# A weave-planned encoder layer on one core: four operations of the second token sums moved into the first Strassen product and from GpSimd to VectorE, one weight remainder moved to VectorE, sample tiles of the retention counted as ready 1.6 planner units later

## The chip, the cores and the metric

The kernel runs on one core of a Trainium2 chip. The metric is device time in microseconds (us), the median of the runs. The core has five engines that run side by side and meet at semaphores: TensorE (PE, matmuls; PEld is its weight load), VectorE (DVE), ScalarE (ACT), GpSimd (POOL) and SyncE (SP, which issues most DMAs). Each engine works through its own queue in order: an instruction that waits holds up everything behind it on that engine.

## The reference, cut to what matters

One layer of a streaming encoder, for 1024 prompt tokens and 32 sample tokens with the same weights:

```
h  = x @ w_in                      # attention q/k/v, indexer, retention q/k/v/gate, two branch gates
A  = sparse attention of h         # top-k keys per query by an indexer score, softmax, times v
R  = retention of h                # rotary q/k, per chunk: scores, state update, group norm, swish gate
m  = sigmoid(g_A) * (A @ w_pa) + sigmoid(g_R) * (R @ w_pr)
x1 = LN(alpha*x + m @ w_o)
y  = LN(alpha*x1 + (silu(x1 @ w_gate) * (x1 @ w_up)) @ w_down)
```

Matmuls run in a rounded fp32 form on operands that are split into a high part and a remainder (`split`, L144): high by ACT, remainder by DVE or POOL as `src - high`.

## The kernel before, in words

**Order of the work.** The order of TensorE's instructions is written out by the kernel. A main stream (a generator of matmuls) is walked by the class `Weave` (L51); side streams, spawned on the way, are let in between two matmuls once the planner's clock `W.t` has reached the time that they asked for. The clock counts planned costs only: a matmul of n columns costs max(256, n)/2400 units (384 columns 0.16, 288 columns 0.12, 512 columns 0.213), and `W.on(engine, cost, after)` books a slot on an engine and returns its end plus a lag (0.3 for ACT, 0.4 for POOL; for DVE 1.6 in this stage). The order on DVE, ACT and POOL is made by the framework's scheduler from program order, readiness and free tile buffers.

**Retention** (`ret_job`, L678). For four weight groups p and nine token tiles t (t = 8 is the sample tile of 32 tokens) the main stream makes one projection (L182 to L198) and spawns `ret_tile` (L560). A prompt tile's projection is copied by ACT (L693), and its ready time is the end of that copy. A sample tile's is merged by ACT and DVE (L201 to L207), and its ready time is only `W.t + 0.2`. `ret_tile` then has four operations of POOL (rotary, L574 to L577) and its steps on PE. These are the times that it asks for:

```
yield 0.0, W.on("p", 2.4, t_ev) + 2.2              # L578, ahead of the transposes L580, L581
yield 0.22, W.on("a", 0.65, W.t + 0.22) + 1.2      # ahead of the scores, L593
yield 0.43, max(W.on("v", 0.5, W.t + 0.43) + 1.0, state_t.get(p, 0.0))   # ahead of L604 to L610
yield c, tt + 5.0                                  # c = 1.3; ahead of the last transposes, L642
```

**Gate projections as filler** (`g_jobs`, L702). 16 blocks b of three chunks (384, 384 and 288 columns, 24 matmuls each, L172) follow the retention as main stream. The weights of block b + 1 are loaded and split when block b begins; block 0's remainder is made by DVE, the others' by POOL. At the start of a chunk, when no side stream is left, `to_attention` (L743) opens the attention, whose two streams are spawned at the start of a later chunk (`t_go = W.t + 1.5`). From then on the gate chunks fill PE between the steps of the attention. Block 15 is kept until the attention has ended.

**Feed-forward.** The first pair of gate and up blocks is made plainly (`u_plain`, L1141), in two halves u of the tokens (264 columns each). All others are made as seven Strassen products for each half (`products`, L1204, 12 matmuls each, numbered z = 0 to 6). The right sides are sums of token blocks, made once by `sums(u)` (L1116): for each of four slices k it forms four block sums and four differences, and splits four results into `tq[2]`, `tq[3]`, `tq[1]` and `T4` (which overwrites the block `B12`). It uses the tiles `e1`, `u2`, `u3`, with two buffers each, which `products` uses for its own evictions too. The block sum of `B21` is made by POOL into a tile `ts` with one buffer (L1121). `sums(0)` runs while `u_plain` is in its second half; all of `sums(1)` follows it, and `products(q, 0, ...)` and `products(q, 1, ...)` come behind that. In `products` the bank of z = 0 is written again by z = 4, after ACT's copy of `e1` (L1222); that of z = 2 by z = 5, after the eviction L1226; that of z = 3 by z = 6. The products of half 1 read `tq[2]`, slice by slice, from z = 1 on.

Of the kernel before, what the change touches and what calls it, by code (L numbers as in the profile page):

```python
# [10 lines left out]
F32 = mybir.dt.float32  # L11
# [3 lines left out]
ALU = mybir.AluOpType  # L15
# [7 lines left out]
HALF, SUB = 528, 264  # L23
# [81 lines left out]
def body(ctx, tc, nc, a):  # L105
# [20 lines left out]
    def f32(ap):  # L126
        return ap.bitcast(F32)

    def dma(out, in_):
        nc.sync.dma_start(f32(out) if out.dtype == F32R else out, f32(in_) if in_.dtype == F32R else in_)  # L130
# [9 lines left out]
    ring1 = Open("ring1", bufs=4)  # L140
# [3 lines left out]
    def split(hi, lo, src, hi_eng="pool", lo_eng="pool"):  # L144
        if hi_eng == "pool":
            nc.gpsimd.tensor_scalar(hi, src, 1.0, 1.0, op0=ALU.mult, op1=ALU.mult)
        elif hi_eng == "act":
            nc.scalar.activation(hi, src, AF.Copy)  # L148
        else:
            nc.vector.tensor_copy(hi, src)  # L150
        e = nc.gpsimd if lo_eng == "pool" else nc.vector
        e.tensor_tensor(lo, src, f32(hi), op=ALU.subtract)  # L152

    def unit(src, p, hi_eng="act", lo_eng="pool"):
        raw = ring1.tile([128, 1024], F32, name="raw", bufs=2)
        dma(raw, src)
        hi = p.tile([128, 1024], F32R, name="whi")
        lo = p.tile([128, 1024], F32R, name="wlo")
        split(hi, lo, raw, hi_eng, lo_eng)
        return hi, lo  # L160

    def blk(u, n=128):
        return tuple(w.rearrange("p (k c) -> p k c", c=n) for w in u)
# [92 lines left out]
    for c0, n in CHUNKS:  # L256
        for k in range(KT):
            for w, raw, i, k0 in ((w0, raws[0], 2, k), (w1, raws[1], 0, k - 1)):
                if c0 == 0 and k0 in pieces:
                    s = slice(pieces[k0][0] * 128, pieces[k0][1] * 128)  # L260
# [22 lines left out]
    ks = ip.tile([128, 1568], F32R, name="iks")  # L283
# [226 lines left out]
    st = {}  # L510

    def load_pair(p, u):
        rg = ring2 if p in (1, 3) else ring1
        src = a["wv"][u] if p == 0 else a["wr"][p - 1, u]
        units.setdefault(p, []).append(blk(unit(src, rg, lo_eng="pool" if p < 2 else "dve"), 512))
# [162 lines left out]
    def ret_job():  # L678
        for p in range(4):
            for t in range(9):  # L680
                if p == 3 and t == 1:
                    ring2.close()
                    st["hA"] = Open("headA")
                if p == 3 and 1 <= t < 6:
                    load_head(0, t - 1)
                if p < 3 and t < 4:
                    load_pair(p + 2, t)
                    W.on("v", 1.2, W.on("a", 0.95, W.t + 0.5))
                qkv = rp.tile([128, 512], F32, name="qkv", bufs=3)
                src = yield from nat_tile(units[p + 1], t, rp, qkv)  # L690
                t_ev = W.t + 0.2
                if t < 8:
                    nc.scalar.activation(qkv, src, AF.Copy)  # L693
                    t_ev = W.on("a", 0.5, W.t)
                    src = qkv
                W.spawn(ret_tile(p, t, src, t_ev))
            units.pop(p)

# [3 lines left out]
    def g_jobs():  # L702
        w = blk(unit(a["wT"][19], ring1, lo_eng="dve"))
        for b in range(16):
            cur = w
            if b < 15:
                w = blk(unit(a["wT"][20 + b], ring1, lo_eng="dve" if b < 1 else "pool"))
            dd = ga_d[b] if b < 8 else gr_d[b - 8]
            for c0, n in CHUNKS:
                if "att" not in st and not W.sides and b >= PRE:  # L710
                    to_attention()
                    t_go = W.t + 1.5
                elif "att" in st and st["go"] and W.t >= t_go:
                    for z in st["go"]:
                        W.spawn(z)
                    st["go"] = None
                if b == 16 - POST and c0 == 0:
                    c_units.append(blk(unit(a["w_pr"][0], ring1)))
                    c_units.append(unit(a["w_pa"][0], ring1))
                while b >= 16 - POST and "rt" not in st:  # L720
                    yield 0.2
                o = gbank()
                yield from tform(o, cur, KT, xr(c0, n), n)
                g = gv.tile([128, 384], F32, name="gev", bufs=2)
                if "rt" in st:
                    nc.vector.tensor_copy(g[:, :n], o[:, :n])
                    dma(dd[:, c0:c0 + n], g[:, :n])
                else:
                    nc.scalar.activation(g[:, :n], o[:, :n], AF.Copy)
                    nc.scalar.dma_start(dd[:, c0:c0 + n], g[:, :n])  # L730
                W.on("a", 0.4, W.t)
# [283 lines left out]
    op = Open("wo", side="right")  # L1015
# [66 lines left out]
    B11, B12, B21, B22 = x1[0][0], x1[0][1], x1[1][0], x1[1][1]  # L1082
# [30 lines left out]
        for i in range(2):  # L1113
            split(hi[:, i], lo[:, i], v[:, i], "act", "dve")

    def sums(u):  # L1116
        s = slice(u * SUB, (u + 1) * SUB)
        for k in range(4):
            a_, b_, c_ = (st["up"].tile([128, SUB], F32, name=nm, bufs=2) for nm in ("e1", "u2", "u3"))
            d_ = st["up"].tile([128, SUB], F32, name="ts", bufs=1)  # L1120
            nc.gpsimd.tensor_tensor(d_, f32(B21[0][:, k, s]), f32(B21[1][:, k, s]), op=ALU.add)  # L1121

            def whole(out, b):
                nc.vector.tensor_tensor(out, f32(b[0][:, k, s]), f32(b[1][:, k, s]), op=ALU.add)

            def cut(t, src):
                split(t[0][:, k, s], t[1][:, k, s], src, "act", "dve")

            whole(a_, B11)
            whole(b_, B12)  # L1130
            nc.vector.tensor_tensor(a_, b_, a_, op=ALU.subtract)
            whole(c_, B22)
            nc.vector.tensor_tensor(b_, c_, b_, op=ALU.subtract)
            nc.vector.tensor_tensor(c_, c_, a_, op=ALU.subtract)
            cut(tq[2], c_)
            cut(tq[3], b_)
            cut(tq[1], a_)
            nc.vector.tensor_tensor(c_, d_, c_, op=ALU.subtract)
            cut(T4, c_)

    def u_plain():  # L1141
        ws = [(went_of(a["w_gate"][f]), went_of(a["w_up"][f])) for f in range(2)]
        sg = hg.tile([128, 2, TT], F32, name="sg", bufs=2)
        while len(W.sides) > 4:
            yield 0.2
        for u in range(2):
            if u == 1:
                while W.sides:
                    yield 0.2
                ynp.close()  # L1150
                st["tset"] = Open("tset")
                for z in range(1, 4):
                    tq[z] = [st["tset"].tile([128, 4, HALF], F32R, name=f"T{z}{i}") for i in range(2)]
                st["up"] = Open("up", side="right")
                sums(0)
                st["quad"] = make(*seq[0])
            s = slice(u * SUB, (u + 1) * SUB)
            for f in range(2):
                wg, wu = (blk(w) for w in ws[f])
                for h in range(2):  # L1160
                    d = sg[:, f, h * HALF + u * SUB:h * HALF + (u + 1) * SUB]

                    def rx(k):
                        b = x1[k // 4][h]
                        return b[0][:, k % 4, s], b[1][:, k % 4, s]
                    pg, pu = mbank(), mbank()
                    yield from tform(pg, wg, KT, rx, SUB)
                    nc.scalar.activation(d, pg[:, :SUB], AF.Silu)
                    yield from tform(pu, wu, KT, rx, SUB)
                    nc.vector.tensor_tensor(d, pu[:, :SUB], d, op=ALU.mult)  # L1170
        sums(1)
        st["quad"].more()
        st["quad"].last()
        store_h(sg, 0)
# [77 lines left out]
    def u_jobs():  # L1252
        nxt = st["quad"]
        for x, (m, f) in enumerate(seq):
            q = nxt
            if m == 0:
                sg = hg.tile([128, 2, TT], F32, name="sg", bufs=2)
            if x + 1 < len(seq):
                nxt = make(*seq[x + 1])
                hooks = {1: nxt.more, 3: nxt.last}  # L1260
            else:
                first.append(went_of(a["w_down"][0]))
                first.append(went_of(hd_d[0], "dve"))
                hooks = {1: lambda: first.append(went_of(a["w_down"][1])),
                         3: lambda: first.append(went_of(hd_d[1], "dve"))}
            yield from products(q, 0, sg, m == 0, {})
            yield from products(q, 1, sg, m == 0, hooks)
            if m == 1:
                store_h(sg, 2 * f)
# [206 lines left out]
```

## Time and profile before

| what | value |
|---|---|
| median of 3 runs | 1900.14 us (1900.13 to 1900.14) |
| profiled execution, its own time | 1900.51 us |
| span of that execution, first to last instruction | 1898.9 us |
| PE, DVE, ACT, POOL busy | 98%, 68%, 38%, 40% |
| mean granted TensorE clock | 0.994 of full speed |

A busy PE is one with a matmul in its pipeline. A timeline row gives start, duration, engine, line, operation and tiles, and in brackets how long the engine stood idle before it and what released it. A windows row gives the length of a stretch, each engine's busy time with its instructions, the granted clock as a share of full speed, and the DMA's share.

### The profile page before, as it was taken

The page shows a single profiled execution, that of the slowest core. Times are in us where ns is not written, and L with a number is a line of the kernel's source. Part 1 is how long each engine was busy: PE and PEld are TensorE (multiplying, and loading weights), DVE is VectorE, ACT ScalarE, POOL GpSimd, SP SyncE. Part 2 cuts the span into 40 slices and gives each one's busy share as a digit, 9 for nine tenths or more (in the row PEclk, how much of TensorE's full clock was granted, in tenths as well). Part 3 has the DMA queues.
Part 4 walks back from the last instruction along what each step waited for, and adds up shares of the span by engine and source line. Part 5 has one row for each costly group of instructions (what it writes and reads, how often), then busy time and mean ns, then how long its engine had stood idle before and what let it go on. Part 6 is the DMA issues. An engine that isn't in the chain of part 4 may idle for free. (4 is left out here: it accounts for less than half of the span.)

```text
span 1898.9 us, 31028 instructions
## 1 busy us (share of the span) xinstructions
PE 1859.0 (98%) x11361; PEld 1688.2 (89%) x11361; DVE 1298.4 (68%) x2693; ACT 715.1 (38%) x1495; POOL 751.8 (40%) x787
## 2 busy tenths in 40 slices
PE   8999999999999999999999999899999999999998
PEld 8999899787888999998999879899999999877776
DVE  4599889999995776676533378754555555476667
ACT  5443322423333555555522255432333332432212
POOL 5445633455545544543321133243343333462211
PEclk9999999999999999999999999999999999999999
DMA  5335742223334756551845662212222222642212
GB/s 189 113 128 196 266 138 86 65 73 98 87 86 125 195 144 171 143 145 52 273 146 155 186 199 84 67 68 67 80 96 71 75 82 90 203 165 89 83 40 91
DMA packets 154367, 233.11 MB, mean 123 GB/s; under 512 B 18960, under 2 KB 118280, under 8 KB 154216
## 3 DMA queue, kind: packets, MB, share of 16 engines
q1 hardware_dynamic: 147736, 223.03, 37.6%
q10 hardware_dynamic: 6480, 8.11, 1.3%
q8 instruction: 89, 1.46, 0.3%
q14 instruction: 62, 0.51, 0.1%
HBM read 164.79 MB, written 67.48 MB: 122 GB/s over the span
## 5 line engine op out<-in xcount | busy, mean ns | idle before, releaser
L152 POOL TENSOR_TENSOR wlo<-raw,whi 128x1024 fp32r<-128x1024 f32 (+2 forms) x83 | 196.1, 2367 | 337.8 <-ACT whi L148 295.2
L148 ACT ACTIVATE whi<-raw 128x1024 fp32r<-128x1024 f32 (+1 forms) x158 | 137.1, 881 | 183.8 <-PE m L1218 33.7
L172 PE MATMUL g<-xh,whi 128*128 128x384 f32 (+1 forms) x600 | 198.2, 330 | 0.0
L172 PE MATMUL g<-xl,whi 128*128 128x384 f32 (+1 forms) x600 | 198.1, 330 | 0.0
L172 PE MATMUL g<-xh,wlo 128*128 128x384 f32 (+1 forms) x600 | 197.9, 330 | 0.0
L377 DVE MAX8 m<-sc 128x8 f32<-128x384 f32 (+6 forms) x209 | 182.2, 874 | 4.7
L378 DVE MATCH_REPLACE8 sc<-m,sc 128x384 f32<-128x384 f32 (+6 forms) x209 | 180.0, 862 | 0.1
L778 POOL TENSOR_TENSOR P<-TB,mask 128x512 f32<-128x512 f32 (+3 forms) x112 | 99.1, 913 | 120.9 <-PE m L842 98.3
L172 PEld LDWEIGHTS g<-xl,whi 128*128 128x128 f32 x600 | 113.5, 189 | 3.0 <-issue 0.9
L172 PEld LDWEIGHTS g<-xh,wlo 128*128 128x128 f32 x600 | 113.5, 189 | 2.4 <-issue 0.5
L172 PEld LDWEIGHTS g<-xh,whi 128*128 128x128 f32 x600 | 113.5, 189 | 2.2
L1315 DVE TENSOR_TENSOR yo<-m,yo 128x512 f32<-128x512 f32 x128 | 85.4, 686 | 43.5 <-PE m L172 42.1
L1218 PE MATMUL m<-T,whi 128*128 128x264 f32 x624 | 114.6, 283 | 0.0
L172 PE MATMUL g<-whi,xl 128*128 128x512 f32 x256 | 104.9, 410 | 0.0
L172 PE MATMUL g<-whi,xh 128*128 128x512 f32 x256 | 104.4, 408 | 0.0
L172 PE MATMUL g<-wlo,xh 128*128 128x512 f32 x256 | 104.4, 408 | 0.0
L1218 PEld LDWEIGHTS m<-T,whi 128*128 128x128 f32 x624 | 96.6, 188 | 0.0
L172 PE MATMUL m<-rT,whi 128*128 128x384 f32 (+1 forms) x384 | 90.7, 322 | 0.0
L1218 PE MATMUL m<-T,wlo 128*128 128x264 f32 x312 | 88.6, 284 | 0.0
L1218 PE MATMUL g<-x,whi 128*128 128x264 f32 x416 | 79.2, 287 | 5.6 <-ACT e L1222 5.6
L1218 PE MATMUL m<-x,whi 128*128 128x264 f32 x416 | 78.5, 287 | 1.2 <-DVE u L1226 0.7
L152 DVE TENSOR_TENSOR wlo<-raw,whi 128x512 fp32r<-128x512 f32 (+1 forms) x81 | 69.6, 872 | 14.0 <-ACT whi L148 13.1
(333 smaller groups left out, 5493.4 us busy)
## 6 DMA issues: line engine op xcount, KB each, us to landing
raw<-wT SPq DMA_DIRECT2D x33, 512.0 KB, 3.7
raw<-w_gate SPq DMA_DIRECT2D x22, 512.0 KB, 3.4
raw<-w_up SPq DMA_DIRECT2D x22, 512.0 KB, 3.4
hd<-sg SPq DMA_DIRECT2D x22, 512.0 KB, 3.2
raw<-w_down SPq DMA_DIRECT2D x22, 512.0 KB, 3.5
raw<-hd SPq DMA_DIRECT2D x22, 512.0 KB, 3.6
raw<-wr SPq DMA_DIRECT2D x16, 512.0 KB, 4.2
ml<-mtd SPq DMA_DIRECT2D x16, 512.0 KB, 4.5
```

Of the source, the lines that this page charges most:

```text
L148: nc.scalar.activation(hi, src, AF.Copy)
L152: e.tensor_tensor(lo, src, f32(hi), op=ALU.subtract)
L172: nc.tensor.matmul(out, lhsT=l, rhs=r, start=i == 0, stop=i == m - 1)
L377: nc.vector.max(m8[0:n], v)
L378: nc.vector.match_replace(v, m8[0:n], v, TAKEN)
L778: nc.gpsimd.tensor_tensor(pp[0:n, n0:n0 + nn], TB[0:n, b0 + n0:b0 + n0 + nn], masks[t][0:n, n0:n0 + nn], op=ALU.add)
L1218: nc.tensor.matmul(o, lhsT=w[l][:, k, :], rhs=b[r][:, k, s], start=z < 4 and k == 0 and j == 0, stop=k == 3 and j == 2, skip_group_check=True)
L1315: nc.vector.tensor_tensor(y, src, y, op=ALU.add)
```

## The change

The sample tiles' ready time in the retention is counted 1.6 units later. The remainder of gate block 1's weights is made by DVE. `sums` takes a list of slices; the sum of `B21` is made by DVE into the tile `u2`, which is free by then, and `ts` is gone (for both halves). `sums(1)` makes slices 0 and 1 ahead of the first Strassen product; slices 2 and 3 are issued in the first product of half 0, behind its evictions z = 1 and z = 2.

```diff
                     src = qkv
+                else:
+                    t_ev += 1.6
                 W.spawn(ret_tile(p, t, src, t_ev))
...
-                w = blk(unit(a["wT"][20 + b], ring1, lo_eng="dve" if b < 1 else "pool"))
+                w = blk(unit(a["wT"][20 + b], ring1, lo_eng="dve" if b < 2 else "pool"))
...
-    def sums(u):
+    def sums(u, ks=range(4)):
         s = slice(u * SUB, (u + 1) * SUB)
-        for k in range(4):
+        for k in ks:
             a_, b_, c_ = (st["up"].tile([128, SUB], F32, name=nm, bufs=2) for nm in ("e1", "u2", "u3"))
-            d_ = st["up"].tile([128, SUB], F32, name="ts", bufs=1)
-            nc.gpsimd.tensor_tensor(d_, f32(B21[0][:, k, s]), f32(B21[1][:, k, s]), op=ALU.add)
...
             cut(tq[1], a_)
-            nc.vector.tensor_tensor(c_, d_, c_, op=ALU.subtract)
+            whole(b_, B21)
+            nc.vector.tensor_tensor(c_, b_, c_, op=ALU.subtract)
             cut(T4, c_)
...
-        sums(1)
+        sums(1, range(2))
...
-            yield from products(q, 0, sg, m == 0, {})
+            yield from products(q, 0, sg, m == 0, {z: (lambda k=z: sums(1, [k + 1])) for z in (1, 2)} if x == 0 else {})
             yield from products(q, 1, sg, m == 0, hooks)
```

## Rows read from the trace of the kernel before

**Rows 1.** The page: the span, and the busy time of the engines.
```profile
span 1898.9 us, 31028 instructions
PE 1859.0 (98%) x11361; PEld 1688.2 (89%) x11361; DVE 1298.4 (68%) x2693; ACT 715.1 (38%) x1495; POOL 751.8 (40%) x787
```

**Rows 2.** The waits of PE over the whole span, the two longest: who waited for whom, us in total, times, longest.
```profile
PE m L580 <- POOL qk L577: 5.8, 3, 2.8
PE g L1218 <- ACT e L1222: 5.6, 1, 5.6
```

**Rows 3.** The timeline of PE in the retention, at the transposes of the sample tiles of p = 0, 1 and 3 (the matmuls of 32x32), with two matmuls of the main stream in a row ahead of the second.
```profile
378.16 0.24 PE L580 MATMUL m<-ident,qk 32*128 32x32 f32 x1 [1.08 <-POOL qk L577]
...
445.80 0.39 PE L172 MATMUL g<-whi,xl 128*128 128x512 f32 x1
446.02 0.39 PE L172 MATMUL g<-whi,xh 128*128 128x512 f32 x1
448.32 0.24 PE L580 MATMUL m<-ident,qk 32*128 32x32 f32 x1 [1.91 <-POOL qk L577]
...
588.08 0.24 PE L580 MATMUL m<-ident,qk 32*128 32x32 f32 x1 [2.82 <-POOL qk L577]
```

**Rows 4.** The timeline of POOL at the sample tile of p = 3.
```profile
584.86 2.35 POOL L152 TENSOR_TENSOR wlo<-raw,whi 128x1024 fp32r<-128x1024 f32 x1 [0.26 <-ACT whi L148]
587.17 0.45 POOL L576 TENSOR_TENSOR qk<-qk,t 32x128 f32<-32x128 f32 x1
587.59 0.44 POOL L577 TENSOR_TENSOR qk<-qk,t 32x128 f32<-32x128 f32 x1
```

**Rows 5.** The timeline of DVE there: a weight remainder of the same size made by DVE, and the last operation of the top-k search.
```profile
578.58 1.22 DVE L152 TENSOR_TENSOR wlo<-raw,whi 128x1024 fp32r<-128x1024 f32 x1
...
589.59 1.34 DVE L379 TENSOR_SCALAR mask<-sc 128x1024 bf16<-128x1024 f32 x1
```

**Rows 6.** The timeline of PE where the retention ends: the last transposes of the sample tile of p = 3, the first matmul of the next gate chunk, the first matmul of the attention.
```profile
608.95 0.31 PE L642 MATMUL m<-ident,on 32*128 32x32 f32 x2
...
609.47 0.29 PE L172 MATMUL g<-xh,whi 128*128 128x288 f32 x1
...
612.84 0.22 PE L788 MATMUL m<-KS,QS 128*128 128x128 f32 x1
```

**Rows 7.** Windows of the attention: with filler, and after the filler has run out; then the first of them for the filler's line alone (PE, PEld).
```profile
612.70:879.50 266.80, 261.74 (x1758) 250.74 (x1758) 184.91 (x652) 145.69 (x381) 127.37 (x121) 1.00 0.57 152
879.50:900.90 21.40, 16.82 (x94) 13.36 (x92) 16.49 (x51) 12.87 (x33) 3.67 (x3) 0.84 0.14 40
...
612.70:879.50 266.80, 187.87 (x937) 150.66 (x936) 1.00 0.57 152
```

**Rows 8.** The waits of PE from 612 to 700 us, the start of the attention.
```profile
PE m L866 <- ACT ph L148: 1.3, 1, 1.3
PE m L867 <- DVE pl L152: 0.6, 2, 0.4
```

**Rows 9.** Windows (PE, PEld, DVE, ACT, POOL busy, granted clock): most of the second half of the plain pair, the first product of half 0, that of half 1; then five us behind PE's stall in the first.
```profile
1183.00:1204.00 21.00, 21.00 (x175) 21.00 (x174) 20.35 (x53) 10.15 (x25) 5.37 (x5) 1.00 0.23 76
...
1204.30:1223.47 19.17, 13.10 (x88) 12.58 (x86) 13.91 (x29) 6.61 (x16) 6.70 (x6) 0.82 0.08 28
1223.47:1233.70 10.23, 10.23 (x86) 10.23 (x85) 4.75 (x9) 4.32 (x9) 1.68 (x1) 1.00 0.31 97
...
1215.00:1220.00 5.00, 3.55 (x14) 3.24 (x15) 4.40 (x13) 2.50 (x8) 0.75 (x1) 0.50 0.07 23
```

**Rows 10.** The timeline of PE in the first product of half 0.
```profile
1215.99 0.81 PE L1218 MATMUL g<-x,whi 128*128 128x264 f32 x2 [5.60 <-ACT e L1222]
...
1219.46 0.81 PE L1218 MATMUL m<-x,whi 128*128 128x264 f32 x2 [0.47 <-DVE u L1226]
```

**Rows 11.** The timeline of ACT ahead of the copy that PE waited for.
```profile
1212.56 0.23 ACT L148 ACTIVATE hs<-sg 128x32 fp32r<-128x32 f32 x1 [2.29 <-DVE sg L1170]
...
1214.89 0.77 ACT L148 ACTIVATE T<-u 128x264 fp32r<-128x264 f32 x2 [1.23 <-DVE u L1133]
1215.56 0.37 ACT L1222 ACTIVATE e<-g 128x264 f32<-128x264 f32 x1
```

**Rows 12.** The timeline of DVE there.
```profile
1203.75 0.42 DVE L152 TENSOR_TENSOR T<-e,T 128x264 fp32r<-128x264 f32 x1
1204.09 0.42 DVE L1131 TENSOR_TENSOR e<-u,e 128x264 f32<-128x264 f32 x1
1206.43 1.50 DVE L1138 TENSOR_TENSOR u<-ts,u 128x264 f32<-128x264 f32 x1 [1.91 <-POOL ts L1121]
1207.86 1.78 DVE L152 TENSOR_TENSOR wlo<-raw,whi 128x512 fp32r<-128x512 f32 x1
...
1212.10 0.42 DVE L1170 TENSOR_TENSOR sg<-m,sg 128x264 f32<-128x264 f32 x1
```

**Rows 13.** The timeline of POOL there.
```profile
1203.14 2.54 POOL L1182 TENSOR_TENSOR qs<-raw 128x512 f32<-128x512 f32 x1 [7.78 <-DVE e L1124]
1205.63 0.77 POOL L1121 TENSOR_TENSOR ts<-x,x 128x264 f32<-128x264 f32 x1
1206.35 1.30 POOL L1183 TENSOR_TENSOR qs<-qs,raw 128x512 f32<-128x512 f32 x1
```

**Rows 14.** The waits of DVE from 1160 to 1225 us, the longest: us in total, times, longest.
```profile
DVE u L1138 <- POOL ts L1121: 3.2, 3, 1.9
```

## The prediction

> **What bounds the kernel now.** The page first: PE is busy for 1859.0 of 1898.9 us, all other engines far less [rows 1]. Time can come only from the 40 us in which PE stands, or from stretches at the lower clock. So the second view is the list of PE's waits. Two entries lead it and both lie where the change works: the transposes L580 wait for POOL, 5.8 us in three places, and one matmul of the Strassen products waits 5.6 us for an ACT copy [rows 2]. The PE timeline shows that the three are sample tiles (the matmuls are 32x32): 1.08 us at p = 0, 1.91 at p = 1, 2.82 at p = 3 [rows 3]. The windows show what the fourth costs in all: the first product takes 19.17 us where its twin of half 1, with the same matmuls, takes 10.23 [rows 9]. The difference, 8.94 us, is 5.60 and 0.47 us of waiting [rows 10] and some 2.9 us of matmuls at half speed: behind the stall the granted clock is 0.50, the level of 1.2 GHz [rows 9]. Pool of gain: 5.8 + 8.9 = 14.7 us.
>
> **Sample tiles, 1.6 units later: 5.5 us less.** The transposes are let in where the planner believes POOL to be done. A unit is real work in PE's queue: a 512-column matmul counts 0.213 units and takes 0.22 us [rows 3], so 1.6 units put PE's arrival about 1.65 us later while it does other work. At p = 0 that clears 1.08 us, at p = 1 all but 0.25 of the 1.91. At p = 3 1.65 of 2.82 us would go by it; the rest goes by the weight edit, since a remainder of 2.35 us stands on POOL between the halves of the rotary [rows 4]. Without it POOL is done some 2 us sooner. Sum: 1.08 + 1.66 + 2.82 = 5.5 us; the ends are 4.0 (POOL's queue orders itself anew and one wait stays in half) and 5.8.
>
> **The remainder on DVE: nothing.** It costs DVE 1.22 us, the price of the same operation there [rows 5]. DVE is filled by the top-k search until 590.9 us [rows 5]; the search ends 1.2 us later. Its masks are first wanted at 612.8 us by the attention [rows 6], so 20 us of cover lie behind it. Without the cover it would be 1.2 us.
>
> **What the later sample tile moves: 2.2 us more.** The last transposes of the sample tile of p = 3 stand one matmul before the end of a gate chunk [rows 6], so the next chunk opens the attention. In the planner's units from the end of that tile's projection, worked through by hand from the costs in the code: before, the four steps are placed at 5.31, 8.65, 12.40 and 23.94, and the chunk ends at 24.32. After, they are due at 6.80, 9.18, 12.82 and 24.28, and the chunk, without the 0.22 of the last step, ends at 24.10. The step falls into the next chunk, the attention opens one chunk later and is let in after a chunk of 384 columns that was its filler before. The filler's weight loads take 150.66 us for 936 matmuls [rows 7], 0.161 us each, 0.175 at 384 columns: the chunk is 24 x 0.175 = 4.2 us. In the filled stretch the attention makes (1758 - 937)/266.8 = 3.1 matmuls a us; after the filler's end, where PE is bound by other engines, 91/21.4 = 4.25 [rows 7]. One chunk less shortens the filled stretch by 266.8 x 4.2/150.66 = 7.4 us; the 23 matmuls of attention that it carried cost 5.4 us in the tail. Net 4.2 - 7.4 + 5.4 = +2.2 us. Ends: +4.2 if the tail goes at the filled pace, +0.9 if those matmuls cost only PE's time (16.82/94 = 0.18 us each). The start gets more lead over PE: two waits of 1.3 and 0.6 us there [rows 8] may go. I take 1.0 us of the 1.9, ends 0 and 1.9, since what they wait for is a chain of ACT, DVE and POOL that keeps its length.
>
> **The sums: 6.3 us less.** Why does PE wait for a copy whose input it finished five us before? ACT's queue. The copy stands behind a small split that waits for DVE, and behind halves of `sums(1)`, slices 2 and 3, which come first in program order [rows 11]. DVE is behind in turn: the last multiplication of the plain pair, possible at 1204.3 us, runs at 1212.1 [rows 12]. It lost 1.91 us waiting for `ts`, which stood on POOL behind an operation of 2.54 us [rows 12, 13]; then a 264-column operation took 1.50 us instead of 0.42 while POOL worked [rows 12, 13].
>
> The edit takes the wait away. It adds eight operations to DVE, four of them in `sums(0)`; back to back one costs 0.34 us (the distance of two starts [rows 12]), 2.75 us in all, against 3.2 us of waits for `ts` in both halves [rows 14]. So DVE's total stays level. The stretch before has no room, 20.35 of 21 us are busy [rows 9], but nothing on PE hangs on it. Slices 2 and 3 now stand behind the copy and behind eviction z = 1, so the copy no longer queues behind them: the 5.60 us and the low clock go.
>
> What is late next. DVE is then 7.8 - 1.9 (the wait) - 1.1 (the slowed operation) - 0.7 (two operations of later slices) + 0.3 (one added) = 4.4 us behind PE instead of 7.8. First, z = 5 writes the bank that eviction z = 2 empties. A product's seventh is 10.23/7 = 1.46 us [rows 9]. Without stalls PE gets there at 1204.3 + 5 x 1.46 = 1211.6; eviction z = 2, due at 1208.8 and 4.4 us late, ends at 1213.2: a stall of 1.6 us. Second, slice 3 needs a `u2` that `products` gives back at its seventh eviction. From there to the remainder of `tq[2]` it is five operations of DVE at 0.34, an ACT half of 0.42 and one more of DVE, some 2.6 us with handovers, and half 1 wants it 2.6 us into its time: with DVE's lag I count 1.0 us. What remains is 2.6 of 8.94, gain 6.3 us. Both are unseen in the trace; the ends are no stall (gain 8.9) and a stall as long as before with its clock (gain 0). I take the value near no stall, since the rows show DVE's queue shorter by 3.4 us and the copy's place in front. The wait added is slice 3's for `u2`; behind it on DVE are evictions z = 0 and z = 1 of half 1, and PE's z = 4 and z = 5 wait for those only 3 us later.
>
> A rule. The row shows a DVE sum slowed from 0.42 to 1.50 us beside a POOL operation of 1.30 [rows 12, 13]. The Trainium skill (SBUF — State Buffer, Who interferes with whom) says that a VectorE instruction with two SBUF inputs and a GpSimd instruction that reads SBUF lock each other out for the whole instruction. By that rule each `ts` off POOL would give DVE back up to the 0.77 us that it takes there, 3.1 us in half 1, an estimate: the stall of 1.6 us would go and the median come to 1887.9 us.
>
> **Sum.** 1900.51 (the profiled execution) - 5.5 - 1.0 + 2.2 - 6.3 = 1889.9. That execution lies 0.4 us above the median, so the median comes to **1889.5 us**.
>
> **Rivals.**
> - The stall moves into half 1. DVE is full from 1183 us on [rows 9], each added operation is paid at 0.34 us, slices 2 and 3 are done some 5 us after half 1 wants them, and the clock drops again: nothing is gained in the products. For it: 20.35 of 21 us, and nothing of slice 3 can be made ahead any more. Against it: the waits for `ts` weigh as much as the added work. 1900.1 - 5.5 - 1.0 + 2.2 = 1895.8 us, with 2 us either way. Perfetto Trace Analysis (Optimizing Scalar/DVE Operations) in the Trainium skill speaks for it: where DVE is saturated, work may be moved off it, and the change does the reverse.
> - The waits of the sample tiles stay, since POOL's queue is ordered anew and the rotary comes later too. Against it: the merge ahead of it is in no way touched. Only the products gain, and the tail pays: 1900.1 - 6.3 + 2.2 = 1896 us, or 1894 if the attention does not move either.
> - The attention's tail goes at the filled pace, and its start gains nothing: 1889.5 + 2.0 + 1.0 = 1892.5 us.
> - Slower: the in-order queue jams twice. If slice 2 stands ahead of evictions z = 2 and z = 3 on DVE, z = 5 and z = 6 wait for its 13 operations (4.5 us), and slice 3, which can start only after z = 6, holds half 1 in the same way. Two stalls of 8.9 us for one: 1900.1 + 8.9 - 5.5 - 1.0 + 2.2 = 1904.7 us. It decides from a lag of DVE of about 7 us at z = 2, where I count 4.4.
>
> **How the numbers follow.** The forecast has 0.56, with its own range of 1884 to 1894; the stall in half 1 has 0.20, the sample waits that stay 0.08, the tail 0.08, the double jam 0.08. A difference of 0.2% (3.8 us) is about what a measurement of this kernel can tell from no change, so faster means below 1896.3. From the cases: faster 0.55 + 0.10 + 0.05 + 0.07 = 0.77; slower, above 1903.9, 0.08; the rest, 0.15, within. The range of 1883.5 to 1899 takes in the lower bounds of the costs nearly whole (4.0 more from the products and the start) and the stall in half 1; outside are the double jam and a few mixed cases.
>
> **What would show it.** Right: no L580 wait above 0.5 us in the list; the wait for `e` gone, and PE's first product of half 0 at 10 to 13 us with a clock of 1.00; the first attention matmul one 384-chunk later in PE's order and a tail of 26 to 27 us instead of 21.4. Wrong: a wait for DVE's or ACT's halves of `T` or `x` in half 1 of more than 3 us, a clock of 0.50 in the products, a first attention matmul behind the same chunk as before, or new waits of over 3 us in the attention, whose order is made anew.

## The result, and the profile after

The changed kernel takes **1888.9 us** (median of 6 runs, 1886.0 to 1890.3) against 1900.5 of the kernel before in the same comparison: ratio 0.9923, 95% interval 0.9908 to 0.9937 (the ratio is the one on record; the quotient of the two medians is 0.9939). The profiled execution, the slowest of the six, took 1890.32 us, 10.2 less than that of before; 10.6 were forecast (1900.51 to 1889.9). Two later comparisons on a chip where the kernel before took 1902.6 and 1903.4 gave 0.9913 (0.9900 to 0.9927) and 0.9912 (0.9897 to 0.9927). That the first comparison came out within 1 us of the forecast is in part luck: 10.6 us lies below the intervals of all three ratios (the lowest end, 0.63% of 1900.5, is 12.0 us), and the medians of the later two differ by 16.3 and 17.1. Nor is each term right: the sums gave more, the move of the attention cost nothing that shows, and in the first profile some 4 us of the gain went again in later products, which two more profiles of the same kernel do not show.

The page of the changed kernel [rows 1]:
```profile
span 1888.5 us, 31016 instructions
...
PE 1856.2 (98%) x11361; PEld 1685.5 (89%) x11361; DVE 1295.5 (69%) x2702; ACT 713.9 (38%) x1495; POOL 741.7 (39%) x778
```
PE's waits over the whole span (who waited for whom, us in total, times, longest) [rows 2]. The two leaders of before are gone or small; what leads now was below them, or has grown (L845, which is L843 of before: 4.2 us instead of 1.6):
```profile
PE m L306 <- ACT xh L148: 4.2, 1, 4.2
PE m L845 <- DVE P L807: 4.2, 1, 4.2
PE m L1219 <- DVE u L1227: 3.3, 6, 1.8
PE m L869 <- DVE mx L803: 1.8, 1, 1.8
...
PE m L580 <- POOL qk L577: 0.7, 1, 0.7
```
In before:
```profile
PE m L843 <- DVE P L805: 1.6, 1, 1.6
```
PE's timeline at the transposes of the sample tiles of p = 0, 1, 3, then at the end of the retention and at the first attention matmul [rows 3, 6]. Only p = 1 still waits. The last transposes (L642) now stand inside the 288-column chunk, and the attention opens behind one more chunk, as worked out:
```profile
378.51 0.24 PE L580 MATMUL m<-ident,qk 32*128 32x32 f32 x1
...
447.79 0.24 PE L580 MATMUL m<-ident,qk 32*128 32x32 f32 x1 [0.66 <-POOL qk L577]
...
584.97 0.24 PE L580 MATMUL m<-ident,qk 32*128 32x32 f32 x1
...
604.28 0.29 PE L172 MATMUL g<-xh,whi 128*128 128x288 f32 x1
604.42 0.29 PE L172 MATMUL g<-xl,whi 128*128 128x288 f32 x1
604.64 0.30 PE L642 MATMUL m<-ident,on 32*128 32x32 f32 x2
...
612.30 0.22 PE L790 MATMUL m<-KS,QS 128*128 128x128 f32 x1
```
Windows (PE, PEld, DVE, ACT, POOL busy, granted clock): the attention with filler and behind it, then the two products of the first pair [rows 7, 9]. The first product takes 10.28 us at full clock instead of 19.17 at 0.82; the second pays 1.4 us:
```profile
612.20:869.20 257.00, 253.92 (x1717) 244.19 (x1716) 178.77 (x631) 141.47 (x373) 120.05 (x114) 1.00 0.58 154
869.20:894.70 25.50, 19.39 (x111) 16.08 (x109) 21.71 (x71) 14.97 (x39) 7.29 (x7) 0.87 0.13 38
...
1196.34:1206.62 10.28, 10.28 (x87) 10.27 (x86) 9.13 (x24) 5.11 (x13) 1.67 (x2) 1.00 0.16 53
1206.62:1218.22 11.60, 10.74 (x87) 10.33 (x85) 9.58 (x21) 6.44 (x15) 1.61 (x1) 1.00 0.26 87
```
The only waits of PE left in the pair (its timeline in half 1) [rows 10]:
```profile
1209.87 0.39 PE L1219 MATMUL m<-T,mh 128*128 128x264 f32 x1 [0.55 <-ACT T L148]
1210.57 0.39 PE L1219 MATMUL m<-T,mh 128*128 128x264 f32 x1 [0.31 <-DVE T L152]
```
ACT's timeline: the copy (L1223) stands right behind the small split and ahead of the first half of slice 2 [rows 11]:
```profile
1199.96 0.23 ACT L148 ACTIVATE hs<-sg 128x32 fp32r<-128x32 f32 x1 [0.76 <-DVE sg L1171]
1200.10 0.37 ACT L1223 ACTIVATE e<-g 128x264 f32<-128x264 f32 x1
1202.98 0.42 ACT L148 ACTIVATE T<-e 128x264 fp32r<-128x264 f32 x1 [2.51 <-DVE e L1131]
```
DVE's timeline: it even waited 1.85 us for a weight half, the last multiplication (L1171) runs at 1199.5, and eviction z = 2 (L1227) at 1202.9 [rows 12]:
```profile
1197.45 1.10 DVE L152 TENSOR_TENSOR wlo<-qs,whi 128x512 fp32r<-128x512 f32 x1 [1.85 <-ACT whi L148]
...
1199.51 0.42 DVE L1171 TENSOR_TENSOR sg<-m,sg 128x264 f32<-128x264 f32 x1
...
1202.87 0.42 DVE L1227 TENSOR_TENSOR u<-m,u 128x264 f32<-128x264 f32 x1
```
The lead over the profile of before (how much earlier the same matmul starts): 4.7 us at the first of the attention (one chunk of 4.2 us taken out), 6.2 at its last (900.63 and 894.44), 8.0 at the first of the products, 15.5 behind the pair (1233.70 and 1218.22), 11.6 at the last of the products, 10.4 at the end of the span. In the second and third profile of the same kernel it is 14.8 and 15.5 behind the pair, 12.8 and 14.4 at the end.

### The profile page after: what moved, and what is told of

It is laid out like the page before. It is cut to its first block, busy times and chain, and to the rows that moved or that the text cites. A ratio compares the mean times of both kernels' runs of the same rounds, so it can differ in the third digit from the quotient of the medians.

```text
span 1888.5 us, 31016 instructions
## 1 busy us (share of the span) xinstructions
PE 1856.2 (98%) x11361; PEld 1685.5 (89%) x11361; DVE 1295.5 (69%) x2702; ACT 713.9 (38%) x1495; POOL 741.7 (39%) x778
## 5 line engine op out<-in xcount | busy, mean ns | idle before, releaser
L1199 POOL TENSOR_TENSOR raw<-raw,qs 128x512 f32<-128x512 f32 x20 | 32.2, 1608 | 146.8 <-DVE wlo L152 96.3
L794 DVE CUSTOM_DVE_ANT_0 P<-m,P 128x512 f32<-128x512 f32 (+3 forms) x112 | 59.1, 533 | 35.2 <-PE m L792 31.4
```

The costliest lines, as they stand in the source:

```text
L794: nc.vector.tensor_tensor_reduce(out=pp[0:n, n0:n0 + nn], in0=L[0:n, 0:nn], in1=pp[0:n, n0:n0 + nn], scale=1.0, scalar=-3e38, op0=ALU.add, ...
L1199: nc.gpsimd.tensor_tensor(a12, a12, self.s2, op=ALU.subtract)
```

## Experiments

Each kernel is set against the kernel before as timed beside it on the same chip; rows with the same value of "before" belong together. The four rows with 1903.62 come from one chip, all others from another.

| kernel | median us | before us | ratio, 95% interval |
|---|---|---|---|
| shift alone | 1896.92 | 1903.62 | 0.9963, 0.9950 to 0.9976 |
| sums alone | 1896.40 | 1903.62 | 0.9963, 0.9950 to 0.9976 |
| shift and weight | 1894.03 | 1903.62 | 0.9950, 0.9937 to 0.9963 |
| after, attention in place | 1891.33 | 1903.62 | 0.9940, 0.9927 to 0.9953 |
| after, second time | 1886.32 | 1902.60 | 0.9913, 0.9900 to 0.9927 |
| DVE sums without the split | 1902.53 | 1902.60 | 0.9999, 0.9991 to 1.0008 |
| split without DVE sums | 1896.03 | 1902.60 | 0.9964, 0.9952 to 0.9977 |
| after, third scratch set | 1886.48 | 1902.60 | 0.9908, 0.9893 to 0.9923 |
| after, third time | 1886.30 | 1903.35 | 0.9912, 0.9897 to 0.9927 |
| attention in place, again | 1890.19 | 1903.35 | 0.9932, 0.9916 to 0.9948 |
| attention two chunks later | 1887.84 | 1903.35 | 0.9918, 0.9905 to 0.9931 |
| third set, 2.2 at p = 1 | 1885.00 | 1903.35 | 0.9904, 0.9889 to 0.9919 |

### The two halves of the change

Before with `t_ev += 1.6` alone:

> Before plus the shift of 1.6 units alone (no weight edit, no edit of the sums). The attention opens one chunk later here too. By the prediction's terms: the sample tiles gain 1.08 + 1.66 + 1.65 = 4.4 us, since at p = 3 the remainder still stands on POOL and some 1.2 us of the wait stay; the move of the attention costs 2.2, its start gives 1.0: 1.2 to 3.2 us less than before, 1897 to 1899. By the rival from the trace of after (the tail does not grow with the chunk that was moved, and the low clock behind it goes): the sample tiles' 4 us and 3 more, 1892 to 1894.

Before with both edits of `sums` and no other:

> Before plus the edit of the sums alone. By the prediction: 6.3 us less, 1894.2, with a stall of 1.6 us at z = 5 of the first product and 1.0 in half 1. By the trace of after: no stall at z = 5, the pair of products 7.5 us shorter, 1893. If the 3.9 us that after loses again in the later products hang on this edit, the median is 1896 to 1897 and the waits for eviction z = 2 (L1226 of before) grow as they do in after; if they come from chance or from the earlier start, they do not grow here.

Before with `t_ev += 1.6` and `lo_eng="dve" if b < 2`:

> Before plus the shift and the weight remainder on DVE, no edit of the sums. By the prediction's terms: 5.5 + 1.0 - 2.2 = 4.3 us less, 1896. By the trace of after: the plain pair ends 8.0 us earlier, and the first product waits for the copy as before: 1892.5. The wait at p = 3 is gone here and is there in the run without the weight edit: 1 to 1.5 us between the two.

The sums give 7.2 us by the medians, shift and weight 9.6; together 16.8. The whole change gave 16.3 and 17.1 on the other chip, so the halves add up as far as medians of two chips can tell. The shift alone (6.7) and shift and weight gave more than the prediction's terms for them (1.2 to 3.2, and 4.3). In the profile of the sums alone the pair takes 21.8 us, as after; with shift and weight alone 29.3, with the wait of 5.6 us, as before. The shift alone left 1.93 us of the wait at p = 3 (0.9 less than before): counted from the first gate chunk, PE came 1.7 us later, as summed (7.5 us instead of 5.8), but POOL's rotary ended 0.8 us later too (9.4 instead of 8.6). The weight edit took the wait whole; between the two medians lie 2.9 us.

### Which part of the sums edit

Before with the B21 sum on DVE, `sums(1)` whole ahead of the products:
```diff
-            d_ = st["up"].tile([128, SUB], F32, name="ts", bufs=1)
-            nc.gpsimd.tensor_tensor(d_, f32(B21[0][:, k, s]), f32(B21[1][:, k, s]), op=ALU.add)
...
-            nc.vector.tensor_tensor(c_, d_, c_, op=ALU.subtract)
+            whole(b_, B21)
+            nc.vector.tensor_tensor(c_, b_, c_, op=ALU.subtract)
```


> Before plus the B21 sums on DVE alone; all four slices of half 1 are still made ahead of the products. By the prediction's terms DVE gets back the wait of 1.91 and the slowed 1.1 us and pays 1.4 for four operations of half 1, but the copy still stands behind halves of slices 2 and 3 on ACT: its wait shrinks from 5.6 to some 4 us, the clock falls still, the pair takes 26.5 to 28 us instead of 29.3. By the rule of mutual exclusion each of the four gives back up to 0.77 more: wait of some 1 us, no low clock, pair 22 to 24 us. By the rival that DVE is full the added operations eat the gain: pair 29 us or more.

Before with `sums(1, range(2))` and slices 2 and 3 as hooks at z = 1 and 2, the sum left on POOL:

> Before plus the split alone: slices 2 and 3 within the first product, the B21 sums still on POOL. If the copy's place in the queue is what the change mends, the wait of 5.6 us is gone here and the pair takes 22 to 23 us. If it is DVE's lag behind the wait for POOL, eviction z = 2 is some 5 us late still, z = 5 waits 2 to 4 us with the clock at 0.50 behind, and the pair takes 25 to 28 us. By the prediction's own terms, DVE 7.1 us behind: 25 to 26.

The split carries the gain; the move to DVE alone gives nothing that shows (0.9999). Without the split, ACT's timeline has the copy (L1221) behind five halves of later slices, four of which waited for DVE:
```profile
1209.30 0.43 ACT L148 ACTIVATE T<-e 128x264 fp32r<-128x264 f32 x1 [0.77 <-DVE e L1129]
1209.99 0.23 ACT L148 ACTIVATE hs<-sg 128x32 fp32r<-128x32 f32 x1 [0.26 <-DVE sg L1169]
1211.27 0.42 ACT L148 ACTIVATE T<-e 128x264 fp32r<-128x264 f32 x1 [1.05 <-DVE e L1129]
1213.01 0.42 ACT L148 ACTIVATE T<-u 128x264 fp32r<-128x264 f32 x1 [1.31 <-DVE u L1131]
1213.69 0.77 ACT L148 ACTIVATE T<-u 128x264 fp32r<-128x264 f32 x2 [0.27 <-DVE u L1131]
1214.37 0.37 ACT L1221 ACTIVATE e<-g 128x264 f32<-128x264 f32 x1
```
The last multiplication is 4.3 us behind PE there (1209.54 against the products' start at 1205.24; 7.7 before), so DVE did get some time back; but PE waits 3.60 us for the copy and 1.94 for eviction z = 2, the first product's clock falls, and it takes as long as before. PE's timeline there:
```profile
1214.79 0.81 PE L1217 MATMUL g<-x,whi 128*128 128x264 f32 x2 [3.60 <-ACT e L1221]
...
1219.75 0.81 PE L1217 MATMUL m<-x,whi 128*128 128x264 f32 x2 [1.94 <-DVE u L1225]
```
Windows of that first product, and of the one with the split and POOL's sums:
```profile
1205.18:1224.40 19.22, 13.67 (x86) 13.15 (x85) 14.25 (x34) 7.23 (x18) 2.16 (x2) 0.73 0.08 28
```
```profile
1206.66:1218.58 11.92, 10.81 (x86) 10.35 (x86) 9.36 (x22) 4.46 (x11) 4.36 (x4) 1.00 0.14 45
```
With the split alone DVE is 4.8 us behind, a little more than in the run above, and yet no copy is waited for: on ACT it stands right behind the small split. So the copy's place decides, not DVE's lag. The first product's only wait is 1.10 us at z = 5 for eviction z = 2: the stall that was forecast for the whole change comes here. ACT's timeline and PE's with the split alone:
```profile
1211.95 0.23 ACT L148 ACTIVATE hs<-sg 128x32 fp32r<-128x32 f32 x1 [0.26 <-DVE sg L1170]
1212.08 0.37 ACT L1222 ACTIVATE e<-g 128x264 f32<-128x264 f32 x1
```
```profile
1215.33 0.50 PE L1218 MATMUL m<-x,whi 128*128 128x264 f32 x2 [1.10 <-DVE u L1226]
```
The pair takes 22.65 us; the sums on DVE make it 21.8.

### The order of the attention

After with `t_ev += 1.6 if p < 3 else 1.2`, measured twice:

> After, with the shift 1.2 instead of 1.6 units at p = 3 alone: the step falls back into its chunk, and the attention opens behind the same chunk as before. All else as in after. By the prediction the move costs 2.2 less 1.0 for the start: 1 to 2 us faster than after, 1887 to 1888. By the rival (the move gains, since the tail grows by 1.5 us and not 5.4 and the low clock behind it goes) 3 us slower than after: 1892.

> After, with 1.2 units at p = 3, the attention behind the same chunk as in before; once more, to be held against the changed kernel on the same chip. By the prediction's terms 1.2 us less than the changed kernel; by the first traces (attention 4.6 us longer, filler chunk of 4.2 us gone) within 1 us of it; by the medians of the first two calls 3 to 5 us more.

After itself, twice more:

> The changed kernel itself once more, on the chip of the runs below. In its first profile the lead over the kernel before was 15.5 us behind the pair of products and 10.4 at the end; 3.9 us of that went between the pair and the last product. If that belongs to the change, this profile shows the same stretch again at 394 to 395 us; if it is chance, at 391 to 392.5, as in the kernels that hold one part of the change, and the ratio to the kernel before comes out lower than 0.992.

> The changed kernel once more, beside the two kernels that differ from it only in where the attention opens. Expected at 0.991 to 0.993 of the kernel before, as twice so far; the stretch from the first attention matmul to the last 282 to 284 us.

After with the first chance to open the attention passed over:
```diff
-                if "att" not in st and not W.sides and b >= PRE:
+                if "att" not in st and not W.sides and b >= PRE and "late" not in st:
+                    st["late"] = 1
+                elif "att" not in st and not W.sides and b >= PRE:
```


> After, with the attention let in one chunk later still (the first chance to open it is passed over): two chunks of 384 columns behind the place of before. By the prediction's terms each chunk costs 4.2 - 7.4 + 5.4 = 2.2 us: 1889 to 1891 and a tail 5.4 us longer than that of after. By the rival that a chunk moved is worth nothing either way: as after, within 1 us, the attention 4.2 us shorter than after's. If moving it gains: 2 to 4 us less than after.

Windows of the attention with filler and behind it, with the attention in place (second profile), then two chunks later:
```profile
608.20:874.80 266.60, 261.70 (x1758) 250.69 (x1757) 184.99 (x652) 145.54 (x381) 127.17 (x121) 1.00 0.57 152
874.80:896.10 21.30, 16.74 (x94) 13.27 (x92) 16.42 (x51) 12.86 (x33) 3.67 (x3) 0.84 0.12 40
```
```profile
615.60:869.00 253.40, 249.10 (x1684) 238.61 (x1682) 174.80 (x624) 141.31 (x368) 112.39 (x106) 1.00 0.55 152
869.00:896.60 27.60, 20.84 (x119) 17.04 (x119) 23.61 (x78) 15.55 (x44) 11.68 (x12) 0.88 0.12 35
```
Six profiles with the attention in place have 266.3 to 267.7 us with filler and 19.4 to 22.3 behind it; seven with it one chunk later 256.8 to 258.4 and 24.4 to 26.0. By the means the move is +4.2 - 9.0 + 4.4 = -0.4 us, not +2.2, and these ranges are too wide to tell -0.4 from nothing. The second chunk costs 1.4 against the third profile of after (first attention matmul 3.53 later, 5.17 less with filler, 3.00 more behind it), some 2 against the means of the seven, and 1.5 by the medians, with intervals that overlap. In the timed runs the first chunk even gains: 1886.30 against 1890.19, timed side by side, with intervals that overlap (0.9897 to 0.9927 and 0.9916 to 0.9948). By the products' start the profiles show 1.5 of those 3.9 us (means of 1196.6 and 1198.1); where the rest lies stays open.

### The rest of the wait in half 1

After with a third set of `e1`, `u2`, `u3` (`bufs=3`), then with it and `t_ev += 2.2 if p == 1 else 1.6`:

> After, with a third set of the scratch tiles e1, u2, u3 (bufs 3 for 2), so that slice 3 does not wait for the set that the first product gives back at its seventh eviction. If that wait is what stalls half 1 for 1.4 us, half 1 takes 10.2 us instead of 11.6 and the pair 20.5 instead of 21.8. If DVE's total is what holds it, the operations that come earlier stand ahead of evictions z = 2 to z = 4, the stall moves to z = 5 or z = 6 of half 0, and the pair stays at 21.8 or grows to 23 us.

> After, with the third set of scratch tiles and 2.2 units instead of 1.6 at p = 1. The set takes 0.6 us from the pair of products, as in its own run (21.2 us); the shift takes the rest of the wait at p = 1 (0.4 to 0.7 us). Expected 1 to 1.5 us less than after; if the step at p = 1 arrives later without need, or the low clock of the attention's tail decides, the same as after.

The set takes the waits out of half 1 (10.21 us) and lengthens half 0 to 11.02, where PE now waits 0.34 us for eviction z = 3: the pair takes 21.2 instead of 21.8 us, where 20.5 was expected if the wait for the scratch set had been all. The work of slice 3 was moved, not hidden. The shift clears p = 1. The last version is the fastest by its median, 1885.0, but 1.3 us below after, timed beside it, is within the intervals: that it beats the changed kernel is not shown.

## Why the prediction held, point by point

- **Sample tiles, 5.5** (the three terms add up to 5.56). With the attention in place the first attention matmul comes 5.0 and 4.6 us earlier than in the profile of before (607.86 and 608.28 against 612.84). p = 0 and p = 3 are clear; p = 1 kept 0.3 to 0.8 us where 0.25 was left by the sum. That at p = 3 both edits are needed was right: the shift alone took 0.9 of 2.82, not 1.65. What the sum missed is the clock. In the profile of before the clock stayed at 1.00 behind these waits [rows 3], and in the one of the sums edit alone behind 3.38 us too; in the run with the split alone the same wait of 2.76 us at p = 3 was followed by a granted clock of 0.63 (the second window below), in the one with DVE sums alone 3.02 us by 0.63 over the next 8 us. Windows of the split alone from that wait on, then the second of them in before:
```profile
580.00:588.00 8.00, 5.24 (x31) 4.70 (x29) 7.89 (x17) 4.58 (x9) 5.58 (x8) 0.95 0.49 158
588.00:596.00 8.00, 8.00 (x31) 7.33 (x32) 4.24 (x10) 2.05 (x7) 4.19 (x7) 0.63 0.57 187
```
```profile
588.00:596.00 8.00, 7.92 (x47) 7.36 (x48) 4.65 (x12) 3.25 (x10) 5.57 (x10) 1.00 0.56 198
```
  PE is busy throughout that window and does 31 matmuls where the profile of before has 47; the first attention matmul comes 27.7 us behind these transposes instead of 24.8. In such executions a wait of 3 us costs 6. That this is why shift and weight gave 9.6 us by the medians, and 4.3 by the forecast's terms, is shown only in part. Estimated as (1 - clock) x time from the mean granted clock of each run, the executions of before timed beside them lost 11.8 us to the low clock on average, those with shift and weight 10.2: 1.5 us. The move of the attention accounts for another 1.6; the remaining 2 us are within the interval (0.9937 to 0.9963 is 7.0 to 12.0 us). For the whole change the same estimate gives 11.7 and 13.1 us before and 6.6 and 6.4 after, so 5 to 7 us of its 16 to 17 came as clock, of which the forecast had counted 2.9, behind the stall in the products. What decides whether the clock falls behind a given wait, no run here shows.
- **Remainder on DVE, nothing.** Held: 1.28 us on DVE, and no wait for it appears. It is block 2's, not block 1's as the text ahead of the prediction has it: when block b begins, `unit` loads block b + 1, so `b < 1` already gave blocks 0 and 1 to DVE (remainders at 578.58 and 580.90 in before), and POOL's at 584.86 [rows 4] is the one that moved. The prediction's sums do not hang on the number.
- **The move of the attention, +2.2, and its start, -1.0.** This step failed: +1.2 for both was forecast, and the profiles have -0.4. That the order moves by one chunk was right to the matmul. Of attention matmuls the filled stretch lost 17, not 23 (1758 - 1717, less 24 of the filler), and the tail took 4.4 us for them, not 5.4. Also PE's own waits with filler fell from 5.1 to 3.1 us (266.80 - 261.74 and 257.00 - 253.92), which the prediction had not counted there; at the start it had counted 1.0 that did not come (1.9 us of waits before, 2.4 after). A gain lay within the stated bounds only if those of the tail and of the start are taken together (0.9 - 1.9 = -1.0).
- **The sums, 6.3.** Right in mechanism, 7.5 in size (29.3 to 21.8 us for the pair). The copy's place in ACT's queue was the cause, as argued: with DVE 4.3 us behind and the copy behind five halves PE waited for it, with DVE 4.8 us behind and the copy ahead of them it did not. The stall of 1.6 us at z = 5 did not come, since DVE was 3.1 us behind PE at the last multiplication and not 4.4, and eviction z = 2 ended 2.4 us late (1203.29, where the prediction's reckoning has 1200.9 without a lag), just before PE came to z = 5 at 1203.64. Half 1 paid 1.4 where 1.0 was counted.
- **The rule.** The row showed a DVE sum at 1.50 us beside POOL. The run with the sums on DVE and nothing else would, by the Trainium skill (SBUF — State Buffer, Who interferes with whom), have had most of the pair's loss back, 22 to 24 us as it was put for that run; it took 29.4. The rule itself is not refuted: that profile still has DVE sums of 1.52 and 1.51 us, beside POOL's work for the next weights. Taking `ts` off POOL did not take POOL out of DVE's way. DVE's timeline in that run:
```profile
1204.68 1.52 DVE L1137 TENSOR_TENSOR u<-u,u 128x264 f32<-128x264 f32 x1
1206.12 1.51 DVE L1122 TENSOR_TENSOR u<-x,x 128x264 f32<-128x264 f32 x1
```
- **The rivals.** The stall in half 1 came with 1.4 us, not with the 8.9 that would have used up the gain; the double jam did not come. The sample waits stayed at p = 1 alone. The tail took its 17 added attention matmuls in 4.4 us, 3.9 a us, nearer the 4.25 of the forecast than the 3.1 of the filled pace. That work put on a full DVE brings nothing held for the DVE sums alone, not for the split.
- **The signs.** Those of being right came, but for two: one L580 wait is 0.66 us (0.5 was the bound; 0.44 and 0.49 in the other two profiles), and the tail is 24.4 to 25.4 us in the three, not 26 to 27. Two signs of being wrong came as well: a wait of over 3 us in the attention (L845, 4.2 us in all three, 1.6 before), and in the first profile a clock of 0.50 in later products, at 1496.6 to 1500.1 us. The first lies in the tail that is summed above, the second belongs to the next point.
- **Given back later.** Between the pair and the last of the products the first profile of after lost 3.9 us: 394.7 against 390.8. In the second and third it took 392.0 and 391.3, in the kernels with a part of the change 390.8 to 392.4. As the same kernel differs by 3.4 us from one execution to another, most of the loss is not the change's. PE waited 1.77 us there once, for an eviction, with the clock low behind it. Windows of that stretch in the first profile of after, then in the second:
```profile
1488.00:1500.00 12.00, 10.23 (x72) 10.02 (x71) 5.64 (x8) 3.42 (x8) 4.93 (x4) 0.86 0.24 81
```
```profile
1488.00:1500.00 12.00, 11.96 (x99) 11.75 (x98) 6.10 (x9) 4.24 (x10) 4.62 (x4) 1.00 0.24 81
```

## What to carry to other kernels

When an engine waits for an operation whose input is long done, look at what stands ahead of it in its own queue: here moving work behind it gave 6.6 us, while relieving the engine upstream gave nothing. Price a short wait of PE with and without the low clock behind it, since the same wait of 3 us cost 3 in one execution and 6 in another. A change of order that shifts work between a filled stretch and its tail has to be summed over both and over the waits inside, and a few us of it are not predictable from one profile.

## What was not expected of the hardware

The longest wait of PE in the tail, 4.2 us in each profile with the attention one chunk later, is for an operation that stands behind two tiny, slow ones in DVE's queue (L807, which runs at 875.77). Timelines of DVE and of POOL there, in the first profile of after:
```profile
871.73 1.10 DVE L802 TENSOR_TENSOR mx<-mx 128x1 f32<-128x1 f32 x1
872.76 0.15 DVE L806 RECIPROCAL mx<-mx 128x1 f32<-128x1 f32 x1
872.83 2.33 DVE L887 TENSOR_TENSOR av<-av 64x32 f32<-64x32 f32 x1
...
875.77 0.47 DVE L807 TENSOR_SCALAR P<-P,mx 128x512 f32<-128x512 f32 x1
...
876.84 0.14 DVE L802 TENSOR_TENSOR mx<-mx 128x1 f32<-128x1 f32 x1
```
```profile
867.90 4.92 POOL L780 TENSOR_TENSOR P<-TB,mask 128x256 f32<-128x256 f32 x5
872.77 2.35 POOL L152 TENSOR_TENSOR wlo<-raw,whi 128x1024 fp32r<-128x1024 f32 x1
```
Each ends as POOL's operation does (872.83 and 872.82, 875.16 and 875.12), and the first takes 0.14 us five us later; the reciprocal between them, with one input, took 0.15. So here an operation of 64x32 on DVE took as long as POOL's of 128x1024 beside it. The rule of the Trainium skill (SBUF — State Buffer, Who interferes with whom) agrees with these rows. That a remainder of 2.35 us on POOL can thus stand in PE's way was not seen ahead; how much of the 4.2 us it makes was not tried.
